# Idle steps behind GpSimd's inverse roots (the late ones on VectorE), and w_out's first two sums copied out of PSUM, in a fused mLSTM and attention block

## The chip, the cores and the metric

The kernel runs on one core of a Trainium2 chip, in one launch. The metric is the time of an execution in device microseconds, and the median over the runs of a kernel is compared. A profiled execution adds a trace: one row for each instruction of TensorE (PE, with its weight loads as PEld), VectorE (DVE), ScalarE (ACT) and GpSimd (POOL), and for the transfers that SyncE (SP) issues.

## The reference

One layer over 256 tokens of width 2048, all in float32:

```python
mod = silu(c) @ w_ada + b_ada            # 6 rows of 2048: shift1, scale1, gate1, shift2, scale2, gate2
h = rms_norm(x, norm1_w) * (1 + scale1) + shift1
mq, mk, mv, mo, mi, mf, dq, dk, dv = split(h @ w_in)
# group A: mLSTM, 4 heads, chunkwise, then an RMS norm per head and a sigmoid gate
h_ml = rms_norm(mlstm_chunkwise(conv_silu(mq, mk), mv, li, lf), mlstm_norm_w) * sigmoid(mo)
# group B: differential attention, 8 heads, q and k normed per 64 columns, rotary on 16 of them
dq = partial_rope(rms_norm(dq, q_norm_w)); dk = partial_rope(rms_norm(dk, k_norm_w))
o_da = rms_norm(diff_attention(dq, dk, dv, lam), subln_w) * (1 - lambda_init)
x = x + gate1 * (concat(h_ml, o_da) @ w_out)
h = rms_norm(x, norm2_w) * (1 + scale2) + shift2
g, u = split(h @ w_gate_up)
x = x + gate2 * ((silu(g) * u) @ w_down)
```

## The kernel before, in words

**Ticks.** The large products (`w_in`, `w_out`, `w_gate_up`, `w_down`) are cut into 392 ticks. A tick takes one weight tile of 128 x 1024 (raw `r`). ScalarE copies it to a rounded high part `wh`, VectorE subtracts to get the low part `wl`, and TensorE makes 12 products of 128x512 from them (`wh` and `wl` against the high part of the activations, `wh` against the low part; lines L581, L582, L583). A group of 512 output columns holds one accumulator `acc(name, group, ...)` of two PSUM banks; there are two such accumulators (`psA`), and four more banks (`psM`, `misc`) for all other work. Ticks 0 to 95 are `w_in`, 96 to 127 `w_out` (`wo`, four groups of 8 ticks), 128 on `w_gate_up` (`gu`), then `w_down` (`dn`).

**Who sets the order.** No scheduler: the Python program emits every instruction in the order in which it stands on its engine. The class `Plan` keeps a list of works, which are generators. Each half tick (`plan.run`) a work may go one step; `yield 0` ends a step, and `yield 1` or `yield 2` ends one and asks for that many PSUM banks before the next. The plan counts VectorE's and ScalarE's backlog in microseconds and lets no work go on while either is too large; GpSimd's time is not counted. `plan.until(names)` lets half ticks pass, without products, until the named works are done. The `w_ada` gemv is filler: tiles of 512 KB (`ada`), most of them used by one VectorE instruction each (L185). `ADA_PLAN` says how many must at least be used in which stretch of ticks (number, and ticks left free at its end); beyond that `ada_idle` uses more where the backlog allows.

**The roots.** Four norms need an inverse square root of a small tile (`rsqrt_first`, two VectorE instructions for a first guess, then `rsqrt_newton`, three rounds of four GpSimd instructions): q and k of the attention's two halves (tiles `rsq`/`sclq` and `rsk`/`rstk`), the attention's output (`of`, followed by the multiply of `o`), and the mLSTM's output (`mf`, followed by the multiply of `num`). For q a thirteenth GpSimd instruction follows, and VectorE does not need the result at once. For k, `o` and `num` VectorE's multiply follows one or two half ticks behind the root. Each exists for g = 0 and g = 1, so that there are eight roots. What these multiplies make is transposed by TensorE (`tpk`, `ot`, `mt`).

**The attention's and the mLSTM's results** are the activations of `w_out`, in four blocks of rows `kb`: 0 and 1 from the mLSTM (`mix0`, `mix1`), 2 and 3 from the attention. `w_out`'s groups 0 and 1 take blocks 2 and 3 first (group 0: 2, 3; group 1: 2, 3) and then 0 and 1 (group 0: 0, 1; group 1: 0, 1); groups 2 and 3 take all four at once.

**The gate's row.** `gate_rows` (work `rows1`) spreads gate1 over all partitions in four quarters: VectorE makes a diagonal `g1rd`, TensorE multiplies it with ones (`g1rp`), ScalarE copies the result to `g1r`. When a group of `w_out` is complete, `residual` multiplies its accumulator by `g1r` and adds x (VectorE, `reso` and `x0r`...). For that the main loop has, at each group's last tick:

```python
        need = list(t["ready"])
        if t["done"] and t["acc"][0] == "wo":
            need.append("rows1")
        plan.until(need, lambda: ada_idle(VFORCE))
```

Of the kernel before, what the change touches and what calls it, by code (L numbers as in the profile page):

```python
# [14 lines left out]
AF = mybir.ActivationFunctionType  # L15
# [149 lines left out]
def tile_block(ctx, tc, x, c, pos, par, w_ada, w_in, w_gt, w_out, w_gu, w_dn, out):  # L165
# [230 lines left out]
        ts(b.bitcast(I32), x_.bitcast(I32), 1, None, ALU.logical_shift_right)  # L396
        ts(y.bitcast(I32), b.bitcast(I32), -1.0, 1597463007.0, ALU.mult, ALU.add)

    def rsqrt_newton(y, b, x_):
        for _ in range(3):  # L400
            nc.gpsimd.tensor_tensor(b, y, y, op=ALU.mult)
            nc.gpsimd.tensor_tensor(b, b, x_, op=ALU.mult)
            nc.gpsimd.tensor_scalar(b, b, -0.5, 1.5, op0=ALU.mult, op1=ALU.add)
            nc.gpsimd.tensor_tensor(y, y, b, op=ALU.mult)
# [323 lines left out]
    def prep(nm, g):  # L728
        t = proj[(DQ if nm == "q" else DK)[g]]
        dst = (sclq if nm == "q" else rstk)[:, :, g * 8:(g + 1) * 8]  # L730
        tmp = sm.tile([P, 2, 16], F32, name=f"rs{nm}{g}", tag="rs", bufs=3)
        xx, b = tmp[:, :, 0:8], tmp[:, :, 8:16]
        yield 0
        sq = slab(f"sq{nm}{g}")
        act(sq[:], t[:], AF.Square)
        yield 0
        red(xx, sq.rearrange("p (t m d) -> p t m d", t=2, d=64), ALU.add)
        ts(xx, xx, 1.0 / 64, EPS, ALU.mult, ALU.add)
        rsqrt_first(dst, b, xx)
        rsqrt_newton(dst, b, xx)  # L740
        if nm == "q":
            nc.gpsimd.tensor_scalar(dst, dst, 0.125, None, op0=ALU.mult)
            rope_products(nm, t)
        else:
            yield 0
            v = t.rearrange("p (t m d) -> p t m d", t=2, d=64)
            for k in range(2):
                tt(v[:, k], v[:, k], dst[:, k].unsqueeze(2).to_broadcast([P, 8, 64]), ALU.mult)
            yield 0
            rope_products(nm, t)  # L750
        yield 2
        pts = [misc(f"tp{nm}{g}{half}") for half in range(2)]
        for half in range(2):
            transposes4(pts[half], t, half)
        yield 0
        o = (qT if nm == "q" else kT)[g] = slab(f"{nm}T{g}")
        for half in range(2):
            act(tok(o, half), pts[half][:], AF.Copy, scale=None if nm == "q" else wqk[:, 0:1])
        plan.rel(2)
# [71 lines left out]
    def finish_attention(g):  # L831
        tmp = sm.tile([P, 3, 8], F32, name=f"of{g}", tag="of", bufs=2)
        f, b, xx = (tmp[:, i] for i in range(3))
        r, o = (y[g].rearrange("p h t -> p (h t)") for y in (rs0, osq))
        yield 0
        stt(xx, r, EPS, r, ALU.mult, ALU.mult)
        stt(xx, o, 1.0 / 128, xx, ALU.mult, ALU.add)
        rsqrt_first(f, b, xx)
        rsqrt_newton(f, b, xx)
        yield 0  # L840
        yield 0
        ov = osl[g].rearrange("p (h d) -> p h d", h=8)
        tt(ov, ov, f.unsqueeze(2).to_broadcast([P, 8, 128]), ALU.mult)
        yield 2
        pts = [misc(f"ot{g}_{half}") for half in range(2)]
        for half in range(2):
            for j in range(4):
                tr(pts[half][:, j * 128:(j + 1) * 128], ov[:, half * 4 + j])
        yield 0
        hi, lo = slab(f"odh{g}", F32R), slab(f"odl{g}", F32R)  # L850
        for half in range(2):
            act(tok(hi, half), pts[half][:], AF.Copy, scale=subc[:, 0:1])
        yield 0
        for half in range(2):
# [137 lines left out]
    def ml_norm(g):  # L992
        h = slice(2 * g, 2 * g + 2)
        yield 0
        stt(mfx[:, h], mden[:, h], -1.0, mden[:, h], ALU.mult, ALU.max)
        tt(mfx[:, h], mfx[:, h], menm[:, h], ALU.max)
        stt(mfx[:, h], mfx[:, h], EPS, mfx[:, h], ALU.mult, ALU.mult)
        stt(mfx[:, h], mssq[:, h], 1.0 / 256, mfx[:, h], ALU.mult, ALU.add)
        rsqrt_first(mf[:, h], mfb[:, h], mfx[:, h])
        rsqrt_newton(mf[:, h], mfb[:, h], mfx[:, h])  # L1000
        yield 0
        yield 0

    mn = par_("mn")

# [65 lines left out]
    def out_done(g):  # L1071
        def squares():
            yield 0
            for t in range(2):
                square_x(1, g, t)

        def go():
            residual(accs.pop(("wo", g)), rows1, g, xs[g], "o")
            plan.add(f"x2_{g}", squares())
        return go  # L1080

    def turn(stage, heads):
# [128 lines left out]
    mix = lambda kb: mixT[kb]  # L1211
    whole = lambda kbs: [(kb, h) for kb in kbs for h in range(2)]
    mready = lambda kbs: [f"mix{kb}" for kb in kbs]
    for g, kbs in ((0, (2, 3)), (1, (2, 3)), (0, (0, 1)), (1, (0, 1))):
        for kb in kbs:
            visit(("wo", g), kb == 2, kb == 1, mix, w_out[g], f"wo{g}", whole((kb,)), mready((kb,)),
                  out_done(g) if kb == 1 else None)
    for g in (2, 3):
        visit(("wo", g), True, True, mix, w_out[g], f"wo{g}", whole((2, 3, 0, 1)), mready(range(4)), out_done(g))
    split_end(lambda k: None)  # L1220
# [131 lines left out]
    for i, t in enumerate(ticks):  # L1352
        plan.next_half()
        if i == turning + 1:
            turn(4, heads)
        for fn in pending:
            fn()
        pending = []
        if i in (turning - 1, turning):
            turn((i - turning + 1) * 2, heads)  # L1360
        weights_hi(i + AHEAD)
        weights_lo(i + (AHEAD if i == 0 or not LO_LATE or t["split"] is not None else AHEAD - 1))
        weights_dma()
# [12 lines left out]
        need = list(t["ready"])
        if t["done"] and t["acc"][0] == "wo":
            need.append("rows1")
        plan.until(need, lambda: ada_idle(VFORCE))
        products(i, 0)  # L1380
        plan.next_half()
        if i == turning - 2:
            weights_hi(turning + 1)
            weights_lo(turning + 1)
        elif t["split"] is None:
            weights_lo(i + AHEAD)
            plan.run()
# [22 lines left out]
        return next(self.gen)  # L1410


ADA_PLAN = ((0, 12, 3), (1, 16, 4), (2, 28, 0), (3, 8, 0), (4, 4, 0), (5, 4, 0), ("wo", 16, 22), ("f0", 24, 5), ("f1", 32, 5), ("f2", 8, 8))


def _layout(a):
# [68 lines left out]
```

## Time and profile before

| | |
|---|---|
| median of 3 runs | 1230.26 us (1230.19 to 1233.88) |
| the profiled execution | 1227.86 us, of which its span 1226.1 us |
| busy TensorE, VectorE, ScalarE, GpSimd | 1189.7, 851.1, 582.1, 50.4 us |
| TensorE's mean granted clock | 0.992 |
| read from HBM | 310.73 MB, mean 255 GB/s over the span |

The span is the time from the first to the last instruction; 1.8 us of the execution's time lie around it. Matmuls are pipelined and their ends are modelled, so TensorE's busy share says less than its waits and the spacing of its instructions. In the rows, `x <- y` after an engine's name is what ended a wait, a number in brackets is the idle time before an instruction, and a `q` behind an engine's name is its sequencer.

### The profile page before, as it was taken

The page shows a single profiled execution, that of the slowest core. Times are in us where ns is not written, and L with a number is a line of the kernel's source. Part 1 is how long each engine was busy: PE and PEld are TensorE (multiplying, and loading weights), DVE is VectorE, ACT ScalarE, POOL GpSimd, SP SyncE. Part 2 cuts the span into 40 slices and gives each one's busy share as a digit, 9 for nine tenths or more (in the row PEclk, how much of TensorE's full clock was granted, in tenths as well). Part 3 has the DMA queues.
Part 4 walks back from the last instruction along what each step waited for, and adds up shares of the span by engine and source line. Part 5 has one row for each costly group of instructions (what it writes and reads, how often), then busy time and mean ns, then how long its engine had stood idle before and what let it go on. Part 6 is the DMA issues. An engine that isn't in the chain of part 4 may idle for free.

```text
span 1226.1 us, 14849 instructions
## 1 busy us (share of the span) xinstructions
PE 1189.7 (97%) x5590; PEld 955.9 (78%) x5590; DVE 851.1 (69%) x1197; ACT 582.1 (47%) x791; POOL 50.4 (4%) x126
## 2 busy tenths in 40 slices
PE   6999899998999898999999999999999999999998
PEld 2767678777888686788888888888888878888886
DVE  3757968898888998879856667878555454545443
ACT  3754345565666345665444444444444443433342
POOL 1000001205022000000000000000000000000000
PEclk9999999999999999999999999999999999999999
DMA  9898987656578897899755547998655544646471
GB/s 343 320 363 321 376 324 251 252 207 234 183 257 314 315 355 279 307 337 344 276 186 184 188 169 291 353 351 319 233 178 196 189 172 172 225 169 238 157 257 52
DMA packets 63258, 313.81 MB, mean 256 GB/s; under 512 B 6993, under 2 KB 7377, under 8 KB 41169
## 3 DMA queue, kind: packets, MB, share of 16 engines
q1 hardware_dynamic: 63186, 312.86, 69.9%
q8 instruction: 44, 0.72, 0.2%
q14 instruction: 28, 0.23, 0.0%
HBM read 310.73 MB, written 2.10 MB: 255 GB/s over the span
## 4 chain that ended last, share of the span: by engine, by line
PE 77%; DVE 13%; issue 3%; DMA 2%; POOL 2%; ACT 2%; SPq 0%; DVEq 0%; POOLq 0%; ACTq 0%
DVE wl L181 5%; DVE ada L185 4%; DMA ada<-in_w_ada_dram 2%; PE acc('dn', 0)_7816 L583 2%; PE acc('dn', 0)_7816 L581 2%; PE acc('dn', 2)_8616 L583 2%; PE acc('dn', 2)_8616 L581 2%; PE acc('dn', 1)_8236 L583 2%; PE acc('dn', 1)_8236 L581 2%; PE acc('dn', 0)_7816 L582 2%; PE acc('dn', 2)_8616 L582 2%; PE acc('dn', 1)_8236 L582 2%; DVE proj L181 1%; PE gv L216 1%; PE at L220 1%
## 5 line engine op out<-in xcount | busy, mean ns | idle before, releaser
L181 DVE TENSOR_TENSOR wl<-r,wh 128x1024 fp32r<-128x1024 f32 x392 | 473.6, 1221 | 206.6 <-ACT wh L211 206.3
L211 ACT ACTIVATE wh<-r 128x1024 fp32r<-128x1024 f32 x392 | 410.5, 1058 | 391.3 <-DMA r<-in_w_gu_dram 42.1
L185 DVE SCALAR_TENSOR_TENSOR ada<-ada,silc 128x1024 f32<-128x1024 f32 x152 | 183.0, 1217 | 1.7 <-DMA ada<-in_w_ada_dram 1.7
L216 PE MATMUL gv<-ada,early 128*32 128x256 f32 x320 | 25.7, 424 | 11.9 <-DMA ada<-in_w_ada_dram 11.7
L581 PE MATMUL acc('dn', 0)_7816<-wh,aTh 128*128 128x512 f32 x88 | 35.9, 408 | 0.0
L583 PE MATMUL acc('dn', 0)_7816<-wh,aTl 128*128 128x512 f32 x88 | 34.3, 390 | 0.0
L582 PE MATMUL acc('dn', 0)_7816<-wl,aTh 128*128 128x512 f32 x88 | 34.3, 389 | 0.0
L581 PE MATMUL acc('dn', 1)_8236<-wh,aTh 128*128 128x512 f32 x88 | 34.2, 389 | 0.0
L582 PE MATMUL acc('dn', 1)_8236<-wl,aTh 128*128 128x512 f32 x88 | 34.2, 389 | 0.0
L583 PE MATMUL acc('dn', 1)_8236<-wh,aTl 128*128 128x512 f32 x88 | 34.2, 389 | 0.0
L581 PE MATMUL acc('dn', 2)_8616<-wh,aTh 128*128 128x512 f32 x88 | 34.2, 389 | 0.0
L582 PE MATMUL acc('dn', 2)_8616<-wl,aTh 128*128 128x512 f32 x88 | 34.2, 389 | 0.0
L583 PE MATMUL acc('dn', 2)_8616<-wh,aTl 128*128 128x512 f32 x88 | 34.2, 389 | 0.0
L216 PEld LDWEIGHTS gv<-ada,early 128*32 128x32 f32 x320 | 7.8, 113 | 27.3 <-DMA ada<-in_w_ada_dram 16.4
L211 ACT ACTIVATE hx<-pt,modc,gcol 128x256 f32<-128x256 f32 (+1 forms) x36 | 17.4, 535 | 17.7 <-PE pt L220 14.6
L181 DVE TENSOR_TENSOR hl<-hx,hh 128x512 fp32r<-128x512 f32 (+1 forms) x18 | 11.4, 631 | 18.8 <-ACT hh L211 18.7
L211 ACT ACTIVATE pm<-sc,st,sclq 128x256 f32<-128x256 f32 (+1 forms) x32 | 15.9, 513 | 12.0 <-POOL st L785 12.0
L211 ACT ACTIVATE aTh<-at 128x512 fp32r<-128x512 f32 x22 | 12.0, 596 | 20.0 <-PE at L220 20.0
L211 ACT ACTIVATE fp<-fp 128x1024 f32<-128x1024 f32 x6 | 6.4, 1062 | 29.4 <-DVE fp L181 29.4
L582 PEld LDWEIGHTS acc('dn', 0)_7816<-wl,aTh 128*128 128x128 f32 x88 | 16.5, 188 | 4.2 <-issue 1.0
L581 PEld LDWEIGHTS acc('dn', 0)_7816<-wh,aTh 128*128 128x128 f32 x88 | 16.5, 188 | 4.2 <-issue 1.0
L582 PEld LDWEIGHTS acc('dn', 2)_8616<-wl,aTh 128*128 128x128 f32 x88 | 16.5, 188 | 3.5
(958 smaller groups left out, 2985.9 us busy)
## 6 DMA issues: line engine op xcount, KB each, us to landing
ada<-in_w_ada_dram SPq DMA_DIRECT2D x192, 512.0 KB, 5.7
r<-in_w_gu_dram SPq DMA_DIRECT2D x76, 1024.0 KB, 6.3
r<-in_w_dn_dram SPq DMA_DIRECT2D x44, 1024.0 KB, 4.8
r<-in_w_in_dram SPq DMA_DIRECT2D x36, 1024.0 KB, 6.7
r<-in_w_out_dram SPq DMA_DIRECT2D x16, 1024.0 KB, 7.4
r<-in_w_in_dram SPq DMA_DIRECT2D x24, 512.0 KB, 5.9
r<-in_w_gu_dram SPq DMA_DIRECT2D x24, 512.0 KB, 4.3
x<-in_x_dram SPq DMA_DIRECT2D x4, 512.0 KB, 5.9
```

What stands on the lines that cost most here:

```text
L181: nc.vector.tensor_tensor(o, a, b, op=op)
L185: nc.vector.scalar_tensor_tensor(out=o, in0=a, scalar=s, in1=b, op0=op0, op1=op1, accum_out=accum)
L211: nc.scalar.activation(o, a, func, **kw)
L216: nc.tensor.matmul(o, l, r, start=start, stop=stop, **kw)
L220: nc.tensor.transpose(o, a, ident[:])
L581: nc.tensor.matmul(o, ah[:, s], wh[:, r], start=t["start"] and j == 0, stop=False)
L582: nc.tensor.matmul(o, ah[:, s], wl[:, r], start=False, stop=False)
L583: nc.tensor.matmul(o, al[:, s], wh[:, r], start=False, stop=t["stop"] and j == 1)
```

## The change

Four edits.

1. `rsqrt_newton` gets a second form (`now`): the three rounds run on VectorE, three instructions each. It is taken for g = 1 of k, `o` and `num`.
2. For g = 0 of these three the root stays on GpSimd, and 7, 7 and 5 half ticks are left behind it (`behind`) before the multiply, in place of 1, 2 and 2. For g = 1 one half tick is left.
3. `w_out`'s groups 0 and 1 alternate by blocks of rows (block 2 of both, block 3 of both, 0 of both, 1 of both). When one is complete, ScalarE copies its accumulator to an SBUF slab (`wo0`, `wo1`), and the residual from that slab and its squares are a work that waits for `rows1`. Only groups 2 and 3 still need `rows1` at their last tick.
4. `ADA_PLAN`: the 16 tiles due in `w_out` may be spread over four more ticks.

```diff
+    def behind(n):
+        for _ in range(n):
+            yield 0
-    def rsqrt_newton(y, b, x_):
+    def rsqrt_newton(y, b, x_, now=False):
         for _ in range(3):
+            if now:
+                tt(b, y, y, ALU.mult)
+                stt(b, b, -0.5, x_, ALU.mult, ALU.mult)
+                stt(y, b, 1.5, y, ALU.add, ALU.mult)
+                continue
             nc.gpsimd.tensor_tensor(b, y, y, op=ALU.mult)
...
-        rsqrt_newton(dst, b, xx)
+        rsqrt_newton(dst, b, xx, nm == "k" and g == 1)
...
-            yield 0
+            yield from behind(7 if g == 0 else 1)
...
-        rsqrt_newton(f, b, xx)
-        yield 0
-        yield 0
+        rsqrt_newton(f, b, xx, g == 1)
+        yield from behind(7 if g == 0 else 1)
...
-        rsqrt_newton(mf[:, h], mfb[:, h], mfx[:, h])
-        yield 0
-        yield 0
+        rsqrt_newton(mf[:, h], mfb[:, h], mfx[:, h], g == 1)
+        yield from behind(5 if g == 0 else 1)
...
+        def later():
+            kept = slab(f"wo{g}")
+            act(kept[:], accs.pop(("wo", g))[:], AF.Copy)
+            yield 0
+            yield 0
+            residual(kept, rows1, g, xs[g], "o")
+            yield from squares()
         def go():
-            residual(accs.pop(("wo", g)), rows1, g, xs[g], "o")
-            plan.add(f"x2_{g}", squares())
+            if g < 2:
+                w = later()
+                next(w)
+                plan.add(f"x2_{g}", w, ["rows1"])
+            else:
+                residual(accs.pop(("wo", g)), rows1, g, xs[g], "o")
+                plan.add(f"x2_{g}", squares())
...
-    for g, kbs in ((0, (2, 3)), (1, (2, 3)), (0, (0, 1)), (1, (0, 1))):
-        for kb in kbs:
+    for kb in WORDER:                                    # WORDER = (2, 3, 0, 1)
+        for g in (0, 1):
...
-        if t["done"] and t["acc"][0] == "wo":
+        if t["done"] and t["acc"][0] == "wo" and t["acc"][1] >= 2:
...
-ADA_PLAN = (... ("wo", 16, 22), ...)
+ADA_PLAN = (... ("wo", 16, 18), ...)
```

What this does to the order on the engines shows at three places. The first is on VectorE at the root of k, g = 0 (tick 54). `rstk` is the first guess that GpSimd's root starts from, `proj_359<-proj_359,rstk` the multiply that waits for the root's end, `rpk` the rotary products behind it. Before:

```order
L192 TENSOR_SCALAR rstk<-rsk_1877 128x2x8
L181 TENSOR_TENSOR wl_1923<-r_1776,wh_1897 128x1024
L181 TENSOR_TENSOR proj_359<-proj_359,rstk 128x512 x2
L181 TENSOR_TENSOR rpk<-proj_359,rope_kc 128x128 x2
L181 TENSOR_TENSOR rpk<-proj_359,rope_ks 128x128 x2
L181 TENSOR_TENSOR proj_359<-rpk 128x16x8 x2
L181 TENSOR_TENSOR wl_1948<-r_1776,wh_1933 128x1024
```

And the same place now:

```order
L193 TENSOR_SCALAR rstk<-rsk_1877 128x2x8
L182 TENSOR_TENSOR wl_1923<-r_1776,wh_1897 128x1024
L186 SCALAR_TENSOR_TENSOR ada_1_1_1731,gsum<-ada_1_1_1731,silc_125 128x1024
L182 TENSOR_TENSOR wl_1942<-r_1776,wh_1931 128x1024
L186 SCALAR_TENSOR_TENSOR ada_1_2_1755,gsum<-ada_1_2_1755,silc_124 128x1024
L182 TENSOR_TENSOR proj_391<-proj_391,acc('in', 6, 4)_1860 128x1024
L182 TENSOR_TENSOR wl_1965<-r_1851,wh_1954 128x1024
L186 SCALAR_TENSOR_TENSOR ada_1_3_1858,gsum<-ada_1_3_1858,silc_125 128x1024
L182 TENSOR_TENSOR wl_1984<-r_1851,wh_1973 128x1024
L186 SCALAR_TENSOR_TENSOR ada_2_0_1879,gsum<-ada_2_0_1879,silc_124 128x1024
L182 TENSOR_TENSOR wl_2016<-r_1899,wh_1992 128x1024
L182 TENSOR_TENSOR proj_359<-proj_359,rstk 128x512 x2
```

Ten rows of 1024 columns stand between the guess and the multiply, where one stood. The attention's heads 0 to 3, which need this k, start some four ticks later for it.

The second place is on VectorE at the roots of k, g = 1, and of `o`, g = 0 (ticks 76 to 79), where the two stood one behind the other on GpSimd. Before:

```order
L192 TENSOR_SCALAR rstk<-rsk_2519 128x2x8
L185 SCALAR_TENSOR_TENSOR ada_4_0_2407,gsum<-ada_4_0_2407,silc_124 128x1024
L181 TENSOR_TENSOR wl_2633<-r_2447,wh_2614 128x1024
L185 SCALAR_TENSOR_TENSOR of_269<-rs_0_148 128x8
L185 SCALAR_TENSOR_TENSOR of_269<-osq_150,of_269 128x8
L190 TENSOR_SCALAR of_269<-of_269 128x8
L192 TENSOR_SCALAR of_269<-of_269 128x8
L181 TENSOR_TENSOR proj_518<-proj_518,rstk 128x512 x2
L181 TENSOR_TENSOR rpk<-proj_518,rope_kc 128x128 x2
L181 TENSOR_TENSOR rpk<-proj_518,rope_ks 128x128 x2
L181 TENSOR_TENSOR proj_518<-rpk 128x16x8 x2
L181 TENSOR_TENSOR wl_2674<-r_2447,wh_2659 128x1024
```

The multiply of `o` was the next row. Now, from the last of the root's three rounds on:

```order
L182 TENSOR_TENSOR rsk_2461<-rstk 128x2x8
L186 SCALAR_TENSOR_TENSOR rsk_2461<-rsk_2461 128x2x8
L186 SCALAR_TENSOR_TENSOR rstk<-rsk_2461,rstk 128x2x8
L182 TENSOR_TENSOR wl_2633<-r_2451,wh_2625 128x1024
L186 SCALAR_TENSOR_TENSOR of_269<-rs_0_148 128x8
L186 SCALAR_TENSOR_TENSOR of_269<-osq_150,of_269 128x8
L191 TENSOR_SCALAR of_269<-of_269 128x8
L193 TENSOR_SCALAR of_269<-of_269 128x8
L182 TENSOR_TENSOR proj_518<-proj_518,rstk 128x512 x2
L182 TENSOR_TENSOR wl_2672<-r_2505,wh_2641 128x1024
```

The root of k is in VectorE's own queue, and the multiply of `o` stands 21 rows behind the last row of its first guess, nine of them of 1024 columns.

The third place is on TensorE where the last quarters of the gate's row are made. Before, in the middle of group 0's last two ticks (107):

```order
L583 MATMUL acc('wo', 0)_3396<-wh_3637,mll_3575 128x512
L216 MATMUL g1rp_3714<-g1rd_3689,ones 128x512
L216 MATMUL g1rp_3729<-g1rd_3724,ones 128x512
L581 MATMUL acc('wo', 0)_3396<-wh_3660,mlh_3574 128x512
L582 MATMUL acc('wo', 0)_3396<-wl_3673,mlh_3574 128x512
```

And now, the last of them alone (tick 110):

```order
L595 MATMUL acc('wo', 0)_3340<-wh_3691,mll_3652 128x512
L217 MATMUL g1rp_3771<-g1rd_3749,ones 128x512
L593 MATMUL acc('wo', 1)_3420<-wh_3712,mlh_3651 128x512
L594 MATMUL acc('wo', 1)_3420<-wl_3734,mlh_3651 128x512
L595 MATMUL acc('wo', 1)_3420<-wh_3712,mll_3652 128x512
```

The last quarter stands behind group 0's last product, nine ticks ahead of group 2's last tick, and no two quarters follow each other. No half ticks without products are left in the order. On SyncE's queue 120 `ada` tiles are now fetched ahead of the first tile of `w_gate_up`, where it was 125; on VectorE 81 are used ahead of group 3's residual, where it was 85.

More of the change, by code (lines that the diff above doesn't have):

```diff
@@ L56 @@
 SQ0, SQ1 = True, False
+WORDER = (2, 3, 0, 1)
 FPAIRS = 6
@@ L1213, in tile_block @@
     mready = lambda kbs: [f"mix{kb}" for kb in kbs]
-    for g, kbs in ((0, (2, 3)), (1, (2, 3)), (0, (0, 1)), (1, (0, 1))):
-        for kb in kbs:
-            visit(("wo", g), kb == 2, kb == 1, mix, w_out[g], f"wo{g}", whole((kb,)), mready((kb,)),
-                  out_done(g) if kb == 1 else None)
+    for kb in WORDER:
+        for g in (0, 1):
+            visit(("wo", g), kb == WORDER[0], kb == WORDER[3], mix, w_out[g], f"wo{g}", whole((kb,)), mready((kb,)),
+                  out_done(g) if kb == WORDER[3] else None)
     for g in (2, 3):
@@ L1410, in __next__ @@
         return next(self.gen)
-ADA_PLAN = ((0, 12, 3), (1, 16, 4), (2, 28, 0), (3, 8, 0), (4, 4, 0), (5, 4, 0), ("wo", 16, 22), ("f0", 24, 5), ("f1", 32, 5), ("f2", 8, 8))
+ADA_PLAN = ((0, 12, 3), (1, 16, 4), (2, 28, 0), (3, 8, 0), (4, 4, 0), (5, 4, 0), ("wo", 16, 18), ("f0", 24, 5), ("f1", 32, 5), ("f2", 8, 8))
 def _layout(a):
```

## The prediction

> **What bounds the kernel now.** I read the page's head first, then TensorE's waits, the chain, VectorE's timeline around each wait, and the windows around `w_out`. The head:
>
> ```profile
> span 1226.1 us, 14849 instructions
> ...
> PE 1189.7 (97%) x5590; PEld 955.9 (78%) x5590; DVE 851.1 (69%) x1197; ACT 582.1 (47%) x791; POOL 50.4 (4%) x126
> ```
>
> TensorE is busy for 97% of the span. The change adds and removes no product, so it can gain only TensorE's waits and what follows each. The view of waits (us in total, times, longest):
>
> ```profile
> PE gv L216 <- DMA ada<-in_w_ada_dram: 11.7, 13, 1.9
> PE ot L220 <- DVE o L181: 4.2, 1, 4.2
> ...
> PE g1rp L216 <- DVE g1rd L181: 3.5, 1, 3.5
> ...
> PE acc('gu', 4, 0)_4423 L582 <- DVE wl L181: 1.3, 2, 1.0
> ...
> PE tpk L220 <- DVE proj L181: 1.3, 1, 1.3
> PE aT L220 <- ACT pm L211: 0.7, 1, 0.7
> ...
> PE sc L216 <- ACT pm L211: 0.5, 1, 0.5
> ```
>
> The largest, 11.7 us for `ada` at the start, lies before everything that changes. Three are the change's: `tpk` 1.3 (the multiply behind k's first root), `ot` 4.2 (behind the roots of k, g = 1, and of `o`, g = 0), `g1rp` 3.5 (the gate's row, for which `until` stops the products). VectorE's timeline says why the first two arise; the bracket is its own idle time and what ended it:
>
> ```profile
> 224.75 1.29 DVE L181 TENSOR_TENSOR proj<-proj,rstk 128x512 f32<-128x512 f32 x2 [3.39 <-POOL rstk L404]
> ...
> 300.33 1.30 DVE L181 TENSOR_TENSOR proj<-proj,rstk 128x512 f32<-128x512 f32 x2 [2.30 <-POOL rstk L404]
> ...
> 305.62 1.22 DVE L181 TENSOR_TENSOR o<-o,of 128x1024 f32<-128x1024 f32 x1 [1.51 <-POOL of L404]
> ...
> 375.36 1.23 DVE L181 TENSOR_TENSOR o<-o,of 128x1024 f32<-128x1024 f32 x1 [2.66 <-POOL of L404]
> ```
>
> VectorE stands still for GpSimd, and all that is behind the multiply in its queue, weights' low parts included, stands with it. `mf` adds a fifth such wait, quoted below.
>
> A wait of TensorE also costs what comes after it. The chain (start, us, what) has the same work twice, at speed and behind a wait:
>
> ```profile
> 262.85 0.87 PE cvt L220 x8
> ...
> 306.90 1.97 PE ot L220 x8
> 308.87 1.34 PE tpk L220 x8
> ...
> 414.72 1.14 DVE wl L181
> ...
> 418.90 2.02 PE g1rp L216 x2
> 420.92 0.43 PE acc('wo', 0)_3396 L581
> ...
> 422.20 0.36 PE acc('wo', 0)_3396 L581
> 422.55 0.23 PE acc('wo', 0)_3396 L582
> ...
> 989.52 0.86 PE g2rp L216 x2
> ```
>
> Eight transposes take 0.87 us at speed, but 1.97 and 1.34 behind the wait for `ot`; two products of a gate's row take 0.86 us late in the kernel, but 2.02 behind the wait for `g1rp`, and the next products 0.43 and 0.36 where 0.23 is usual. The windows show a lower granted clock at that place (time, then busy PE, PEld, DVE, ACT, POOL, then PEclk, DMA share, GB/s):
>
> ```profile
> 380.00:400.00 20.00, 20.00 (x97) 16.67 (x97) 18.23 (x36) 14.79 (x24) 5.79 (x12) 1.00 0.95 365
> 400.00:420.00 20.00, 16.43 (x64) 11.59 (x63) 19.93 (x36) 5.82 (x7) 0.00 (x0) 0.97 0.84 312
> 420.00:440.00 20.00, 20.00 (x84) 16.09 (x83) 18.16 (x26) 9.50 (x16) 0.00 (x0) 0.94 0.92 329
> 440.00:460.00 20.00, 20.00 (x90) 16.57 (x89) 18.46 (x24) 7.68 (x9) 0.00 (x0) 1.00 0.96 381
> ```
>
> The clock is 0.97 and 0.94 around the wait at 418.90 and 1.00 on both sides of it.
>
> **The change part by part.** *k, g = 0: seven idle half ticks.* GpSimd's rows (start, us):
>
> ```profile
> 220.32 1.12 POOL L401 TENSOR_TENSOR rsk<-rstk 128x16 f32<-128x16 f32 x1 [4.01 <-DVE rstk L192]
> 221.52 0.22 POOL L402 TENSOR_TENSOR rsk<-rsk 128x16 f32<-128x16 f32 x1
> ...
> 224.50 0.22 POOL L404 TENSOR_TENSOR rstk<-rstk,rsk 128x16 f32<-128x16 f32 x1
> ...
> 282.65 0.21 POOL L401 TENSOR_TENSOR rsq<-sclq 128x16 f32<-128x16 f32 x1 [26.56 <-DVE sclq L192]
> ...
> 291.06 1.10 POOL L742 TENSOR_SCALAR sclq<-sclq 128x16 f32<-128x16 f32 x1
> ```
>
> The twelve operations run from 220.32 to 224.72, 4.4 us, with VectorE idle for most of it. Behind idle steps VectorE works on beside them. The nearest row for that is q's root of thirteen, 282.65 to 292.16: 9.5 us, 0.73 each, with single ones of 1.10. So k's root takes between 4.4 and 12 x 0.73 = 8.8 us; I take 8.8. The cover is ten rows of 1024 columns at the `wl` pitch of 1.14 in the chain: 11.4 us. VectorE's wait of 3.39 goes and with it `tpk`'s 1.3. If the cover failed, it would cost at most that 1.3 again. Heads 0 to 3 start some four ticks later; their `mix` blocks are consumed only in `w_out`, some forty ticks on. A: **1.3 us**.
>
> [...]
>
> *k, g = 1, and `o`, g = 0.* The one root goes to VectorE, so that GpSimd no longer has two in a row; the other gets 21 rows of cover, of which nine wide ones alone give 9 x 1.14 = 10.3 us against 8.8. `ot`'s wait of 4.2 goes, and the slow transposes behind it, 1.97 + 1.34 - 2 x 0.87 = 1.57. It could be only the 4.2, if the slow transposes have another reason. B: **5.8 us**.
>
> *`mf`.* For g = 1 the move takes VectorE's 1.49 us, counted below; no wait of TensorE hangs on it. For g = 0 VectorE has no wait now; five half ticks more delay `mix0` within the ticks between its making and its use in `w_out`. Between nothing and one small wait of 0.7: nothing.
>
> *The residuals as later work.* The last quarter of the gate's row now stands in tick 110 and is wanted at tick 119, nine ticks ahead, 24.5 us at 2.72 each (12 products of 0.23), so nothing stops for it. That ends the 3.5 us of `g1rp`, 2.02 - 0.86 = 1.16 for its slow products, and 3 x (0.43 - 0.23) + 0.36 - 0.23 = 0.73 for those behind. C: **5.4 us**; its lower bound is nothing (third rival).
>
> *What is added on VectorE.* 27 small operations for 36 on GpSimd. The nearest rows, six in a chain of dependent ones:
>
> ```profile
> 385.79 0.16 DVE L185 SCALAR_TENSOR_TENSOR mfx<-mden 128x4 f32<-128x4 f32 x1
> ...
> 386.92 1.66 DVE L185 SCALAR_TENSOR_TENSOR num<-num,mf,proj 128x256 f32<-128x256 f32 x4
> ...
> 393.82 1.67 DVE L185 SCALAR_TENSOR_TENSOR num<-num,mf,proj 128x256 f32<-128x256 f32 x4 [1.49 <-POOL mf L404]
> ```
>
> Six starts from 385.79 to 386.92, 1.13 us or 0.19 each: 27 x 0.19 = 5.1 us. VectorE stops losing 3.39 + 2.30 + 1.51 + 2.66 + 1.49 = 11.35 us, and four `ada` (4 x 1.14 = 4.6 us) leave `w_out` for later, so that it has 10.8 us more room ahead of the last residuals, though the windows show it at 18.2 to 19.9 of 20.
>
> *What is added on ScalarE.* Two copies of an accumulator. The nearest row is such a copy later on, and what follows it there:
>
> ```profile
> 495.45 1.03 ACT L211 ACTIVATE fp<-acc('gu', 1, 0)_4261 128x1024 f32<-128x1024 f32 x1 [1.73 <-PE acc('gu', 1, 0)_4261 L583]
> 496.38 1.05 ACT L211 ACTIVATE wh<-r 128x1024 fp32r<-128x1024 f32 x1
> ```
>
> The copy waits 1.73 us for the last product, takes 1.03, and the next `wh` is queued behind it. ScalarE is busy for 5.82 and 9.50 of 20 us in 400 to 440, and `wh` is made two ticks ahead of its use: 2 x 1.03 and two waits of 1.73 make 5.5 us hidden; without that cover TensorE would wait up to 2.8 us twice. The first accumulator's banks are wanted again two ticks (5.4 us) behind its last product; a copy is done after 1.03. Alternating the groups changes no count. Nothing.
>
> *Queues.* On SyncE five `ada` tiles fewer (2.6 MB at 512 KB) are fetched ahead of `w_gate_up`. The four windows move (365 + 312 + 329 + 381) x 20 = 27.7 MB in 80 us; without those tiles and 5.4 us, 25.1 MB in 74.6 us are needed, 337 GB/s, less than the 381 of 440 to 460. On GpSimd nothing but roots is queued, so what it loses delays nobody. The squares of groups 0 and 1 now follow their residuals later; norm 2 waits for groups 2 and 3 anyway.
>
> *The sum.* 1.3 + 5.8 + 5.4 = 12.5 us. Moving the attention by four ticks may bring waits of the kind already there (`aT` 0.7, `sc` 0.5); between none and two of each (2.4) I allow 1.0. The profiled execution, span and 1.8 us around it, is 1227.86, so 1227.9 - 11.5 = 1216.4. It lies 2.4 below the median 1230.26; against the medians the forecast is **1218.8 us**.
>
> **The rivals.** *VectorE becomes the bound.* If it is what sets the pace from `rstk` to `w_out`, as its 19.93 of 20 says, the gain is only its own balance, 11.35 - 5.1 = 6.2: 1224.1. Against it: TensorE waits for `wl` only 1.3 us in all, after `w_out`. Chance 0.10.
>
> *C comes back.* The row is wanted at group 2's end instead, or weights lag without the pause: gain 12.5 - 5.4 = 7.1, 1223.2. The nine ticks and the 337 GB/s speak against it. 0.08.
>
> *GpSimd is blocked in full.* If each of the twelve operations waits for a wide one and takes the 1.10 to 1.12 of the slow rows and its turn, some 1.2, the root takes 14.4 us; k's cover of 11.4 is short by 3.0, VectorE waits about as before (3.39), A's 1.3 is lost, and `o` loses about 1.0 of B: gain 10.2, 1220.1. [...] For it stand the slow rows, against it 0.73 as the mean. 0.06.
>
> *The four banks of `misc` become the bound (slower or no gain).* The heads are packed more tightly between ticks 57 and 102, with some 48 takings of banks. A taking that waits costs about what `aT` waits for `pm`, 0.7 us. 13 such waits bring the gain of 12.5 within 3.7 us (0.3% of 1230, about what a measurement of this kernel can tell from no change); from 24 on it is slower; thirty cost 21.0: +8.5, 1238.8. Against it: one such wait in the whole trace. Within 0.3%: 0.09, which holds too that the waits only move to the next multiply; slower: 0.06.
>
> *More.* If the small waits (`aT`, `sc`, `wl`: 0.7 + 0.5 + 1.3) vanish too, gain 15.0 with no allowance: 1215.3, and clock recovered elsewhere may add 1 to 2 more. 0.05.
>
> **How the numbers follow.** The forecast itself (gain 9 to 15 us) keeps 0.56; its own range is 1215.3 to 1221.3. Faster by over 0.3% are 0.56 + 0.10 + 0.08 + 0.06 + 0.05 = 0.85, the same 0.09, slower 0.06. The range ends below at 1213.5 (the largest gain and its extra), above at 1226.0, near the 0.3% bound, so that it takes in the first three rivals and leaves out the 0.15 of the fourth and the tails.
>
> **What the profile would show.** GpSimd x90 instead of x126 and 35 to 45 us; VectorE some 5 us busier, without the waits for `rstk`, `of` and `mf`; ScalarE with two more copies; among TensorE's waits no `tpk`, `ot`, `g1rp` of over 0.7; the granted clock near 1.00 at 400 to 440; the last root rows between wide VectorE rows, each root under 10 us. It would be wrong if `misc` tiles head the list of TensorE's waits, if products of `wo` wait for `wl` or `wh`, if residuals of group 2 wait for `g1r`, or if the three waits go and the span does not follow.

## The result and the profile after

The changed kernel takes 1211.59 us (median of 4, 1211.11 to 1212.17), the kernel before 1232.07 (median of 4, 1230.19 to 1234.96): ratio 0.9832, 95% interval 0.9818 to 0.9847. The forecast was 1218.8, its range 1213.5 to 1226.0; the time lies below it. Over all runs of the study the medians are 1231.4 (66 executions of before, 1226.5 to 1236.4) and 1212.0 (8 of the changed one, 1211.1 to 1214.3).

The profiled execution took 1212.17 us. Its page:

```profile
span 1210.5 us, 14851 instructions
...
PE 1188.0 (98%) x5590; PEld 956.7 (79%) x5590; DVE 855.7 (71%) x1224; ACT 586.2 (48%) x795; POOL 42.9 (4%) x90
```

VectorE has 4.6 us more work, GpSimd 90 rows in place of 126. ScalarE has four rows more: the two copies, and two more loads of its function table (1.28 us each). TensorE's waits (engine, line, what it waited for; us, times, longest):

```profile
PE gv L217 <- DMA ada<-in_w_ada_dram: 7.7, 9, 2.5
...
PE acc('gu', 0, 0)_4189 L593 <- ACT hh L212: 2.2, 2, 1.1
PE sc L217 <- ACT pm L212: 0.7, 1, 0.7
PE pt L221 <- DVE hx L191: 0.7, 1, 0.7
PE aT L221 <- DVE pm L186: 0.6, 1, 0.6
```

The three waits at which the change was aimed (`ot` 4.2, `g1rp` 3.5, `tpk` 1.3) are gone; `pt` has fallen from 1.3 to 0.7, and the wait for `wl` in the fifth tile of gate_up (1.3) is gone too. The windows around `w_out`, columns as in the prediction:

```profile
380.00:400.00 20.00, 20.00 (x94) 16.32 (x93) 19.42 (x46) 13.30 (x20) 0.00 (x0) 1.00 0.74 266
400.00:420.00 20.00, 20.00 (x88) 15.65 (x87) 18.88 (x32) 10.08 (x14) 0.00 (x0) 1.00 0.87 308
420.00:440.00 20.00, 20.00 (x90) 16.57 (x89) 19.86 (x29) 11.75 (x17) 0.00 (x0) 1.00 0.86 317
440.00:460.00 20.00, 20.00 (x89) 16.54 (x89) 19.96 (x25) 10.16 (x13) 0.00 (x0) 1.00 0.99 384
```

TensorE is busy throughout and its granted clock is 1.00, where it was 0.97 and 0.94. VectorE is as full as 19.96 of 20, and holds nothing up.

To compare traces by place, I take for each TensorE instruction the distance to the next one's start, less the median distance for the same output and shape, and sum it by ticks. This excess holds waits and slow clock together. Ticks 0 to 48, which no edit touches, differ between the profiles of this study by up to 4.3 us, for a reason that is not shown, so I count from tick 48.

| ticks | before, four profiles | after, two profiles | forecast |
|---|---|---|---|
| 54 to 72 (k's first root, heads 0 to 3) | 4.9 to 5.0 | 0.9 | -1.3 (A) |
| 72 to 80 (`ot`) | 5.8 to 7.1 | 0.2 | -5.8 (B) |
| 80 to 96 (heads 4 to 7) | 1.6 to 1.7 | 3.4 | +1.0 (allowance) |
| 104 to 112 (`g1rp`) | 4.1 to 5.8 | 0.1 | -5.4 (C) |
| 120 to 128 (`pt`) | 3.3 to 4.3 | 2.1 | 0 |
| 128 to 136 (gate_up's first tiles) | 1.6 to 4.0 | 1.6 | 0 |
| 136 to 152 (`wl`) | 2.0 | 0.3 | 0 |
| 48 to 200, all | 25.6 to 29.3 (mean 27.0) | 9.2 | -11.5 |

The profile used for the forecast was the shortest of the four from tick 48 on, at 25.6.

### The profile page after: what moved, and what is told of

The parts are those of the page before. It is cut to its first block, busy times and chain, and to the rows that moved or that the text cites. A ratio compares the mean times of both kernels' runs of the same rounds, so it can differ in the third digit from the quotient of the medians.

```text
span 1210.5 us, 14851 instructions
## 1 busy us (share of the span) xinstructions
PE 1188.0 (98%) x5590; PEld 956.7 (79%) x5590; DVE 855.7 (71%) x1224; ACT 586.2 (48%) x795; POOL 42.9 (4%) x90
## 4 chain that ended last, share of the span: by engine, by line
PE 92%; DVE 3%; DMA 2%; issue 1%; ACT 1%; SPq 0%; POOL 0%; DVEq 0%; ACTq 0%; POOLq 0%
DMA ada<-in_w_ada_dram 2%; PE acc('dn', 0)_7811 L595 2%; PE acc('dn', 0)_7811 L593 2%; PE acc('dn', 2)_8611 L595 2%; PE acc('dn', 2)_8611 L594 2%; PE acc('dn', 1)_8231 L595 2%; PE acc('dn', 1)_8231 L594 2%; PE acc('dn', 1)_8231 L593 2%; PE acc('dn', 0)_7811 L594 2%; PE acc('dn', 2)_8611 L593 2%; PE gv L217 2%; DVE ada L186 1%; DVE wl L182 1%; PE at L221 1%; PE apart('dn', 3)_8992 L595 1%
## 5 line engine op out<-in xcount | busy, mean ns | idle before, releaser
L593 PE MATMUL acc('dn', 0)_7811<-wh,aTh 128*128 128x512 f32 x88 | 35.9, 408 | 0.0
L595 PE MATMUL acc('dn', 0)_7811<-wh,aTl 128*128 128x512 f32 x88 | 34.3, 390 | 0.0
L594 PE MATMUL acc('dn', 0)_7811<-wl,aTh 128*128 128x512 f32 x88 | 34.3, 389 | 0.0
L593 PE MATMUL acc('dn', 1)_8231<-wh,aTh 128*128 128x512 f32 x88 | 34.2, 389 | 0.0
L594 PE MATMUL acc('dn', 1)_8231<-wl,aTh 128*128 128x512 f32 x88 | 34.2, 389 | 0.0
L595 PE MATMUL acc('dn', 1)_8231<-wh,aTl 128*128 128x512 f32 x88 | 34.2, 389 | 0.0
L593 PE MATMUL acc('dn', 2)_8611<-wh,aTh 128*128 128x512 f32 x88 | 34.2, 389 | 0.0
L594 PE MATMUL acc('dn', 2)_8611<-wl,aTh 128*128 128x512 f32 x88 | 34.2, 389 | 0.0
L595 PE MATMUL acc('dn', 2)_8611<-wh,aTl 128*128 128x512 f32 x88 | 34.2, 389 | 0.0
L212 ACT ACTIVATE fp<-fp 128x1024 f32<-128x1024 f32 x6 | 6.4, 1062 | 29.3 <-DVE fp L182 29.3
L182 DVE TENSOR_TENSOR hl<-hx,hh 128x512 fp32r<-128x512 f32 (+1 forms) x18 | 11.4, 631 | 12.3 <-ACT hh L212 12.1
L594 PEld LDWEIGHTS acc('dn', 0)_7811<-wl,aTh 128*128 128x128 f32 x88 | 16.5, 188 | 4.2 <-issue 1.0
```

Source lines behind the costliest of these rows:

```text
L182: nc.vector.tensor_tensor(o, a, b, op=op)
L212: nc.scalar.activation(o, a, func, **kw)
L593: nc.tensor.matmul(o, ah[:, s], wh[:, r], start=t["start"] and j == 0, stop=False)
L594: nc.tensor.matmul(o, ah[:, s], wl[:, r], start=False, stop=False)
L595: nc.tensor.matmul(o, al[:, s], wh[:, r], start=False, stop=t["stop"] and j == 1)
```

## The experiments

The first question was which part of the change carries the gain, and whether the parts add.

**Edits 1 and 2 alone.** `w_out`'s order, its residuals and `ADA_PLAN` are those of before:

```diff
-    rsqrt_newton(...)              # as before, all on GpSimd
+    rsqrt_newton(..., g == 1);  yield from behind(7, 7 or 5 if g == 0 else 1)
```

> Edits 1 and 2 alone (roots on VectorE, idle steps); w_out in the old order, residuals at once, 16 tiles over 22 ticks. If the parts add: A + B = 7.1 us off the median of before (about 1231), so 1224, less up to 5 us if the gate's row is later for the later attention (the order now lets eight half ticks pass for it, where there were four); TensorE's waits for ot and tpk gone, the one for g1rp kept at 3.5 us or longer. If VectorE is the bound, the gain is 6.2 - C or less: over 1228. If the excess over my forecast comes from the attention, the median is under 1220.

Measured: 1226.75 us, ratio 0.9967 (0.9952 to 0.9982). Up to tick 96 the trace is that of the changed kernel, and at tick 104 it is 7.2 us ahead of before's, near A + B (7.1). By the excess it is 6.3: 9.6 less up to tick 80, and 3.3 more in ticks 80 to 104, so the match with A + B is in part chance. Then the excess of ticks 104 to 112 is 9.7 us, where before has at most 5.8. TensorE's waits:

```profile
PE g1rp L217 <- DVE g1rd L182: 5.1, 2, 3.3
...
PE pt L221 <- DVE hx L191: 2.9, 1, 2.9
...
PE acc('wo', 0)_3340 L595 <- DVE mll L186: 1.2, 1, 1.2
PE acc('wo', 0)_3340 L595 <- DVE odl L186: 1.1, 1, 1.1
```

VectorE's timeline there, between two quarters of the gate's row:

```profile
411.01 0.69 DVE L182 TENSOR_TENSOR g1rd<-ident,modc 128x512 f32<-128x512 f32 x1
411.62 1.22 DVE L186 SCALAR_TENSOR_TENSOR ada<-ada,silc 128x1024 f32<-128x1024 f32 x1
...
412.76 1.22 DVE L186 SCALAR_TENSOR_TENSOR ada<-ada,silc 128x1024 f32<-128x1024 f32 x1
...
414.22 1.23 DVE L186 SCALAR_TENSOR_TENSOR ada<-ada,silc 128x1024 f32<-128x1024 f32 x1 [0.23 <-DMA ada<-in_w_ada_dram]
...
415.37 0.69 DVE L182 TENSOR_TENSOR g1rd<-ident,modc 128x512 f32<-128x512 f32 x1
```

Three rows of filler stand between two quarters, the last after a wait for its own transfer. Two products of group 0 also wait, at ticks 98 and 106, for the low parts of the attention's and the mLSTM's results (`odl`, `mll`), which they don't in before or in the changed kernel. Most of what edits 1 and 2 gain is paid back there. That the attention ends later, and the gate's row with it, is not enough to explain it: with the idle steps alone (below) heads 0 to 3 start as late, and ticks 104 to 112 have 0.8. Why three of the row's four quarters stand at tick 107 here is not shown.

**Edits 3 and 4 alone.** All roots and idle steps as before:

```diff
+    if g < 2: copy the sum to a slab; residual and squares as a work behind rows1
+    for kb in WORDER: for g in (0, 1): ...
-    ("wo", 16, 22)
+    ("wo", 16, 18)
```

> Edits 3 and 4 alone; roots and idle steps as before. If the parts add: C = 5.4 us off the median of before (about 1231): 1225.6; the wait for g1rp gone, those for ot (4.2) and tpk (1.3) kept; executions still spread over some 5 us if long waits of TensorE make the spread, over 1 us if the pause for the gate's row alone made it. If the gain of the stage behind it (the low parts of gate_up's fifth tile, 1.7 us, and the row's end) hangs on these edits, 1222 to 1224. If the products would only wait elsewhere: within 1 us of before.

Measured: 1224.47 us, ratio 0.9942 (0.992 to 0.9965). The excess of ticks 104 to 112 is 0.4; `ot` and `tpk` wait as before. So C was sized well. But 4 us (edits 1 and 2) and 7 us (3 and 4) make 11 by the ratios, and the whole change makes 19 to 21: the parts don't add. Edits 1 and 2 alone have 9.7 us in ticks 104 to 112, and edit 3 on top of them leaves 0.1.

**Edit 4 undone** in the changed kernel:

```diff
-    ("wo", 16, 18)
+    ("wo", 16, 22)
```

> The changed kernel with edit 4 undone (16 tiles over 22 ticks). If the waits decide, within 1 us of the changed kernel (1211.6). If the excess over the forecast (3 us between the end of w_out and the eighth tile of gate_up in the profiles) comes from fewer w_ada tiles on VectorE ahead of it, 1213.5 to 1215.

Measured: 1213.1 us (1211.95 to 1214.94). From tick 48 to the end its trace differs from the changed kernel's by 0.04 us. Edit 4 does nothing there, and the median lies within the changed kernel's own executions (1211.1 to 1214.3).

**The gate's row asked for again** at all four groups, in the changed kernel:

```diff
-    if t["done"] and t["acc"][0] == "wo" and t["acc"][1] >= 2:
+    if t["done"] and t["acc"][0] == "wo":
```

> The changed kernel, but all four groups of w_out ask for the gate's row at their last tick, as before; sums still copied, groups alternate. If the pause is what cost C: TensorE waits for g1rp or next to it by 1 to 4 us, with slow products behind, 1213 to 1217, and the executions spread over more than the 1.1 us of the changed kernel. If C's gain is the copies and not the pause: within 0.5 us of 1211.6.

Measured: 1215.84 us; from tick 48 it takes 2.9 us longer than the changed kernel, with copies and alternation unchanged:

```profile
PE g1rp L217 <- DVE g1rd L182: 1.6, 1, 1.6
```

So the pause costs time also when it is only two half ticks: 1.8 us at ticks 104 to 112, the rest where a product of gate_up waits for `wl` again (1.0).

Beside the kernel with edits 1 and 2 alone, this one shows more. Both ask for the row at all four groups, but ticks 104 to 112 have 9.7 us there and 1.9 here. The two differ in the copies, in edit 4 and in the alternation, which moves group 0's last tick, where the row is first asked for, from 107 to 109; the row's last quarter stands at 107 there and at 109 here. So with edits 1 and 2 in place, most of what edit 3 gains is there although the row is still asked for at every group.

**Before, without filler in the pause:**

```diff
-        plan.until(need, lambda: ada_idle(VFORCE))
+        plan.until(need, lambda: None)
```

> The kernel before, where nothing of w_ada is taken up during the half ticks that pass for the gate's row (the order had two w_ada rows, 2.3 us, between each two of the row's quarters there). If that filler is what makes the pause, TensorE's wait for g1rp of 3.5 falls under 1 us, the products behind it run at 0.23, and 4 to 5 us are gained: 1225.5 to 1226.5 against 1230.6 of before, as by edit 3 alone (1224.5). If the row's own chain sets the pause: 1229 to 1231.

Measured: 1225.99 us, ratio 0.9959 (0.9944 to 0.9974), 4 to 5 us as expected, though not in the way expected:

```profile
PE g1rp L216 <- DVE g1rd L181: 2.4, 1, 2.4
```

The wait falls by 1.1 us only. By tick 112 the gain against before's second profile is 2.5 us; the rest comes behind it, where `pt` waits 0.7 in place of 1.3 and the wait for `wl` in gate_up moves and shrinks. Filled with other work this pause is longer than empty (the wait for `g1rp` is 3.5 us against 2.4), and the order behind it changes too.

**Edit 2 alone, for g = 0, and edit 1 alone.** `w_out` is as before in both. First the idle steps (7, 7, 5) with all roots on GpSimd:

```diff
-    rsqrt_newton(dst, b, xx, nm == "k" and g == 1)   # edit 1 undone, likewise for of and mf
+    rsqrt_newton(dst, b, xx)
```

> Edit 2's idle steps alone for g = 0 (7, 7, 5); all roots on GpSimd, g = 1 with the old steps; w_out as before. If idle steps are enough for A but k's and o's roots on GpSimd one behind the other need edit 1, A's 1.3 us plus VectorE's room up to tick 72 as in the changed kernel (7 us at tick 64), and a part of B: TensorE's wait for tpk gone, that for ot left at 1 to 3 us. The gate's row costs a pause of one half tick by the order, where there were four: the end at 1221 to 1227. If edit 1 alone carries B, the wait for ot stays at 4.

Measured: 1221.33 us, ratio 0.9916 (0.9896 to 0.9936). `ot` doesn't wait at all, which I had expected at 1 to 3 us; `tpk` (1.7) and `sc` (1.6) do. Then edit 1 with the old steps for g = 0:

```diff
-    yield from behind(7 if g == 0 else 1)
+    yield from behind(1 or 2)                        # as before
```

> Edit 1 alone: roots of k, o and num, g = 1, on VectorE; g = 0 on GpSimd with the old steps; w_out as before. If the two roots one behind the other were B, TensorE's wait for ot falls from 4.1 to under 2 us and its slow transposes go, 3 to 6 us off before's median of about 1231; the wait for tpk (1.3) and the pause for the gate's row (two half ticks, where there were four) stay: 1224 to 1228. If idle steps are needed for it: 1229 to 1231.

Measured: 1218.89 us, ratio 0.9904 (0.9885 to 0.9923), 5 us better than the best I had expected. `ot` waits 1.1 us, `g1rp` 1.5. Either edit by itself gains more than both do without edit 3; ticks 104 to 112 have 0.8 and 1.8 us here, against 9.7 with both.

**B undone:** k's root, g = 1, on GpSimd again, and o's, g = 0, behind it with two half ticks; all else as changed.

```diff
-    rsqrt_newton(dst, b, xx, nm == "k" and g == 1)
+    rsqrt_newton(dst, b, xx)                         # and behind(1)
-    yield from behind(7 if g == 0 else 1)            # of
+    yield from behind(2 if g == 0 else 1)
```

> The changed kernel with B undone: k's root, g = 1, on GpSimd with one idle half tick, and the root of o, g = 0, behind it with two. If term B holds, VectorE waits 2.3 and 1.5 us again, TensorE about 4 us for ot, and the transposes behind it are slow: 5.8 us as in the profile, or 6.7 with the 0.9 us that the second profile of before took longer there: 1217.4 to 1218.3. If long waits of TensorE make executions spread, this kernel's lie over 3 us apart, where the changed kernel's lie within 1.1. If the other terms had been carrying B: under 1215.

Measured: 1218.17 us; from tick 48 it takes 5.7 us longer than the changed kernel, where B was 5.8. VectorE waits 2.9 us for `rstk` and 1.2 for `of` again, but TensorE's loss comes back only in part at `ot`, where I had about 4, so that the equal size is partly chance:

```profile
PE sc L217 <- ACT pm L212: 3.1, 1, 3.1
...
PE ot L221 <- DVE o L182: 2.1, 1, 2.1
```

**A undone:** one half tick behind k's first root.

```diff
-    yield from behind(7 if g == 0 else 1)            # k
+    yield from behind(1)
```

> The changed kernel with the seven idle half ticks behind k's root, g = 0, taken back to one: VectorE waits 3.4 us for GpSimd there again and heads 0 to 3 start some four ticks earlier. If my term A holds, TensorE's wait for tpk of 1.3 returns and nothing more: 1212.5 to 1213.5 against 1211.6. If the later start of the heads is itself a part of the gain (all roots at once on VectorE, which has the early start too, lost 8 us by tick 112), 1215 to 1220, with new waits between ticks 64 and 108.

Measured: 1218.33 us; from tick 48 it takes 6.2 us longer than the changed kernel. Term A was 1.3. 4.0 of it lie in ticks 54 to 72 (`tpk`, and `aT` and `sc` of the heads), and 1.6 in the first tiles of gate_up, behind a wait for `hh` that is as long as the changed kernel's (rows further below). Those 1.6 may be the execution's and not A's; without them it is 4.6. TensorE's waits:

```profile
PE tpk L221 <- DVE proj L182: 2.2, 2, 1.3
PE sc L217 <- ACT pm L212: 1.7, 2, 1.2
PE aT L221 <- ACT pm L212: 0.7, 1, 0.7
```

**All six roots on VectorE**, one half tick behind each:

```diff
-    rsqrt_newton(dst, b, xx, nm == "k" and g == 1)   # likewise of and mf
+    rsqrt_newton(dst, b, xx, nm == "k")
-    yield from behind(7 if g == 0 else 1)
+    yield from behind(1)
```

> The changed kernel with all six roots on VectorE and no idle steps: 27 more VectorE rows, 5.1 us, GpSimd keeps q's two roots alone. If VectorE has room there (it leads by 2 to 8 us at the ticks 96 to 120), 1210 to 1212 as the changed kernel, since no waits remain to be gained. If VectorE's room is short in the attention, 1213 to 1217, with waits for wl or o.

Measured: 1224.57 us, 13 us over the changed kernel, worse than I had expected at worst: without any wait for GpSimd the heads' waits grew (`aT` for `pm` 4.3, `ot` 1.7, `tpk` 1.7).

**Wait for GpSimd, or early heads?** Two kernels take only k's root, g = 0, to VectorE, with the seven half ticks kept and with one:

```diff
-    rsqrt_newton(dst, b, xx, nm == "k" and g == 1)
+    rsqrt_newton(dst, b, xx, nm == "k")              # behind(7 if g == 0 else 1), or behind(1)
```

> The changed kernel with the root of k, g = 0, on VectorE (nine small rows, 1.7 us) and the seven idle half ticks kept: no wait for GpSimd and the late start of heads 0 to 3. If the late start is what term A missed (6.2 us in the run with one half tick, where I had 1.3), the time stays within 2 us of the changed kernel, 1211.5 to 1214, and TensorE's excess between ticks 54 and 72 stays near 0.9. If it was the wait for GpSimd, the same.

> The same with one idle half tick: no wait for GpSimd, but the early start of the heads. If A's 6.2 us were VectorE's wait for GpSimd (3.4) and what follows it, they are gained here too: 1211 to 1214, excess of ticks 54 to 72 at 1 to 2 us. If they are the early heads, it is 1216 to 1219 with an excess of 3 us or more there, in the waits of aT and sc.

Measured: 1218.64 us with seven, where I had expected 1211.5 to 1214, and 1232.20 with one, where I had at most 1219. Neither has a wait for this root. With seven the excess of ticks 54 to 72 stays low, 2.6 us; of the 4.9 us that it loses in all, 1.6 lie there and 2.6 in ticks 96 to 112. With one it is 9.4 us there, more than before's 5.0, by the waits of the heads:

```profile
PE sc L217 <- ACT pm L212: 4.4, 1, 4.4
PE aT L221 <- ACT pm L212: 4.3, 1, 4.3
```

So taking the wait for GpSimd away is not the gain. What the seven half ticks do to the place of the heads is: with one in their place the time is longer by 13.6 us here, and by 6.7 with the root on GpSimd (A undone). Why both kernels are slower with this root on VectorE is not settled: the plan counts VectorE's rows and not GpSimd's, so that these kernels' order differs at many places.

**Three more profiles of before and one of the changed kernel**, for the spread:

> The kernel before, unchanged, for a second profiled execution. Its unprofiled executions run from 1227.4 to 1234.3, the profiled one took 1227.9. If the spread comes from the w_ada transfers of the start, the two profiles differ by 0.3 to 3 us at tick 48 and by the same amount at the end. If it comes from the long waits (ot, g1rp) and the clock behind them, they differ by over 1 us more between ticks 72 and 112.

> The kernel before, third profile. Its timed executions have a median near 1231, its two profiles 1227.9 and 1228.1. If the rest is made in the start by the w_ada transfers and in the clock behind ot, as the first two profiles differ there by 0.6 and 0.9, a longer execution shows 1 to 4 us in the ticks 0 to 48 and nothing elsewhere.

> The kernel before, fourth profile, as the third: if the spread sits in the long waits instead, the ticks 72 to 80 and 104 to 112 differ from the first two profiles by over 1 us.

> The changed kernel once more, for the spread of its executions (four lay between 1211.1 and 1212.2) and a second profile. If spread comes from the w_ada transfers of the start alone, more executions reach 1210 to 1215, as the starts of nine profiles differ by 3.5 us. If waits make it, they stay within 1.5 us. Median 1211 to 1213 either way.

Before took 1228.13, 1231.41 and 1230.34 us in these profiles. From tick 48 they are 0.9, 3.7 and 1.3 us longer than the first, at `ot` (0.3 to 1.3) and in the first tiles of gate_up (up to 3.3); at `g1rp` one of them is 1.7 shorter. The changed kernel's executions (1211.55 to 1214.29, 1214.29 in the profile) have two profiles that differ by 2.1 us up to tick 48 and by 0.04 behind it. Windows of before, the first profile and the fourth:

```profile
480.00:490.00 10.00, 7.20 (x33) 5.47 (x34) 7.41 (x17) 6.87 (x15) 0.00 (x0) 1.00 0.43 179
```

```profile
480.00:490.00 10.00, 6.44 (x24) 4.56 (x24) 6.19 (x16) 6.02 (x16) 0.00 (x0) 0.83 0.50 211
```

Behind waits of nearly the same length (`pt` 1.31 and 1.35 us, `hh` 1.08 in both) the clock was 1.00 in one execution and 0.83 in the other, and the fourth lost 1.6 us there. (In the third profile the clock is 0.66, but `pt` also waits longer, 2.20.) Two kernels show the same: the changed kernel, and below it the one with A undone, wait alike at gate_up's start, and run the products behind it at different speeds:

```profile
468.50 0.50 PE L593 MATMUL acc('gu', 0, 0)_4189<-wh,hh 128*128 128x512 f32 x1 [1.08 <-ACT hh L212]
468.83 0.40 PE L594 MATMUL acc('gu', 0, 0)_4189<-wl,hh 128*128 128x512 f32 x1
469.07 0.39 PE L595 MATMUL acc('gu', 0, 0)_4189<-wh,hl 128*128 128x512 f32 x1
```

```profile
472.49 0.65 PE L593 MATMUL acc('gu', 0, 0)_4180<-wh,hh 128*128 128x512 f32 x1 [1.08 <-ACT hh L212]
472.94 0.63 PE L594 MATMUL acc('gu', 0, 0)_4180<-wl,hh 128*128 128x512 f32 x1
473.37 0.63 PE L595 MATMUL acc('gu', 0, 0)_4180<-wh,hl 128*128 128x512 f32 x1
```

The starts are 0.24 us apart above and 0.43 below, behind the same wait of 1.08.

Of the twelve products behind the first wait for `hh`, none starts over 0.35 us behind the one before in before's first profile, and eight do in its fourth; of the same twelve none does in the changed kernel (0.33 at most), and eight do with A undone (0.42 to 0.45). What sets the clock there is not shown.

## Why the prediction was wrong, point by point

The direction and the mechanism held: the three waits went, the clock came back (1.00 at 400 to 440, where it was 0.97 and 0.94), and no new bound took their place. What failed are two terms and the basis: A, priced at one wait of 1.3 us, where its stage gave 4.0; the stretch behind group 3 of `w_out`, put at nothing, which gave 2.9 (how is open in part); and the distance of one profile from its median, carried over to the changed kernel. The error of 7.2 us (1218.8 against 1211.6) has three parts: 2.4 from the basis, 4.2 from the sum (15.7 between the two profiled executions, where I had 11.5), and 0.6 by which the changed kernel's profile is longer than its median. From tick 48 on the two profiles differ by 16.4, which is 4.9 over my sum: 2.7 by A and 2.9 behind group 3, less 0.8 by more new waits than I allowed; ahead of tick 48 the changed one lost 0.7.

- **The basis.** I set the sum against one profiled execution and moved its 2.4 us below the median on to the changed kernel, which has no such distance. Of four profiles mine was the shortest from tick 48; part of its distance came from time that other executions lose behind waits (1.6 us behind `hh` in the fourth, at a clock of 0.83 in place of 1.00), of which the change removes one (`ot`, 0.3 to 1.3 us between the profiles). The mean of the four is 1.4 us longer. About 1.6 us more of the 19.4 between the medians show in no profile from tick 48 on; where they lie is open.
- **A, the mis-sized term: 1.3 forecast.** Ticks 54 to 72 gave 4.0, and taking the idle steps back costs 6.2 in all, or 4.6 without the lower clock (0.83) at gate_up's start. I priced the one wait behind the multiply and called the four ticks' delay of the heads free, since the heads' results are used late. It was a gain: `aT` and `sc` of heads 0 to 3 no longer wait, but `aT` and `sc` of the heads behind them cost 1.8 more.
- **B, 5.8 forecast:** 5.6 in my profile, 6.9 in the longest; 5.7 when it is undone. Right in size; when it is undone in the changed order, it is shared between `ot` and `sc`.
- **C, 5.4 forecast:** 5.7. Right in size. I had not seen that some 2.5 us of the pause were filler which the plan puts on VectorE ahead of the row it waits for, nor that edits 1 and 2 would stretch that pause (9.7 us in ticks 104 to 112) without edit 3.
- **The allowance, 1.0 for new waits:** 1.8 came in ticks 80 to 96. Right in kind. But behind group 3 of `w_out` I had counted nothing, and 2.9 us came there (`pt` 1.1, `wl` 1.7). I had `wl` only in the rival of the larger gain. Edits 3 and 4 alone remove both (with two new waits for `wl`, 0.9 and 1.0, at other ticks), emptying the pause shortens both, and edit 4 isn't the reason. In every run with edit 3 `pt` waits 0.7, and in the three with edit 1 or 2 but without edit 3 it waits 1.8 to 2.9; so the part at `pt` is edit 3's. That a forced `ada` less in `w_out` leaves VectorE earlier at norm 2 fits with this, but is argued, not shown.
- **VectorE:** +5.1 forecast, 4.6 measured, without becoming the bound. **ScalarE's copies:** they waited 3.9 and 2.9 us for the last product, more than the 1.73 of my row, and stayed hidden:

```profile
416.27 1.02 ACT L212 ACTIVATE wo<-acc('wo', 0)_3340 128x1024 f32<-128x1024 f32 x1 [3.91 <-PE acc('wo', 0)_3340 L595]
...
422.58 1.03 ACT L212 ACTIVATE wo<-acc('wo', 1)_3420 128x1024 f32<-128x1024 f32 x1 [2.91 <-PE acc('wo', 1)_3420 L595]
```

- **k's root behind idle steps:** 8.8 us forecast, under a cover of 11.4; it took 10.4 (221.01 to 231.37), and the multiply started 1.0 us later, without a wait. GpSimd's timeline:

```profile
221.01 1.12 POOL L413 TENSOR_TENSOR rsk<-rstk 128x16 f32<-128x16 f32 x1 [4.01 <-DVE rstk L193]
222.21 1.08 POOL L414 TENSOR_TENSOR rsk<-rsk 128x16 f32<-128x16 f32 x1
...
225.66 0.21 POOL L413 TENSOR_TENSOR rsk<-rstk 128x16 f32<-128x16 f32 x1
...
226.55 0.22 POOL L416 TENSOR_TENSOR rstk<-rstk,rsk 128x16 f32<-128x16 f32 x1
226.85 1.07 POOL L413 TENSOR_TENSOR rsk<-rstk 128x16 f32<-128x16 f32 x1
...
230.30 1.07 POOL L416 TENSOR_TENSOR rstk<-rstk,rsk 128x16 f32<-128x16 f32 x1
```

and VectorE's beside it:

```profile
224.29 1.21 DVE L186 SCALAR_TENSOR_TENSOR ada<-ada,silc 128x1024 f32<-128x1024 f32 x1
...
225.43 1.21 DVE L182 TENSOR_TENSOR proj<-proj,acc('in', 6, 4)_1860 128x1024 f32<-128x1024 f32 x1
226.57 1.28 DVE L182 TENSOR_TENSOR wl<-r,wh 128x1024 fp32r<-128x1024 f32 x1
...
232.37 1.28 DVE L182 TENSOR_TENSOR proj<-proj,rstk 128x512 f32<-128x512 f32 x2
```

Eight of the twelve operations take 1.05 to 1.12 us, one for each wide row of VectorE. The other four, at 0.20 to 0.22, all lie beside the one row that reads one of its inputs from PSUM (`acc`).

The 0.73 on which I relied was a mean over two kinds of operation: of the thirteen in q's root seven took 0.20 to 0.35 us and six 1.05 to 1.30. I had also written that nothing but roots is queued on GpSimd; eight products of the heads (`st`) are, though no wait of TensorE in this trace is for one of them.

Of the rivals, "blocked in full" had eight of the twelve operations right in length (1.05 to 1.12 us, where it had 1.10 to 1.12 for each) and the price wrong: the root took 10.4 us in place of 14.4 and stayed inside its cover, so nothing was lost. VectorE as the bound, C's return and the banks of `misc` did not come. The rival of the larger gain (0.05) came nearest, but not by its own account: of its three waits `wl` went, while `aT` and `sc` moved to later heads (0.6 and 0.7), and with 1215.3, or 1213.5 with more clock, it too was above the measured time.

## What to carry to other kernels

Look at what a pause makes late and what fills it before pricing it: here filler stood in front of the very work that the pause waited for, and the two halves of the change gained 4 and 7 us apart but some 20 together, since one removed the pause that the other lengthened. When a step is moved in a tightly packed order, the waits of the work behind it move too, for better or worse by several times the wait that one aims at, so a term taken from one wait needs a range of that size on both sides. Take the basis from more than one profile where TensorE waits in the middle of a kernel.

## What was not expected of the hardware

A small GpSimd operation took either 0.2 to 0.4 us or about as long as the wide VectorE row beside it. In the first profiles of before and after, 64 GpSimd operations of the roots and heads overlapped a VectorE row of 512 or 1024 columns with two SBUF inputs. 50 of them took 1.05 to 1.47 us beside rows of 1.21 to 1.28 (one, beside two such rows in turn, 2.25), four took 0.52 to 0.57 beside rows of 512 columns (0.68 to 0.69), and the other ten, 0.20 to 0.38, had all started before the row did. Of 112 others (no such row, or one with a PSUM input) none took over 0.38. And the clock behind waits of about 1 us differed from execution to execution: 1.00 or 0.83 over the same 10 us of the same kernel, worth 1.6 us.
